# A decoder trunk on one core: q, k and v formed in pairs by seven block products for eight, with h and N kept in DRAM meanwhile

## The chip, the cores and the metric

The kernel runs on one core of one Trainium2 chip. The metric is the time of one execution on the device in microseconds (us). A core has five engines that work beside each other, each through a queue of its own in order: TensorE (PE; PEld is its loading of weights), VectorE (DVE), ScalarE (ACT), GpSimd (POOL) and SyncE (SP), which here only issues transfers. SBUF is the core's working memory, PSUM the accumulators into which TensorE writes, in banks of 128 x 512 float32, and DRAM the chip's memory. Transfers (DMA) run beside all engines.

## What is computed

A trunk of two layers on 1024 positions of width 1024, in float32. Layer 0 mixes positions by a gated MLP on chunks, layer 1 by dilated attention; each is followed by a squared-ReLU MLP of width 4096, with RMSNorm ahead of each part and at the end. The attention is what the change touches: 8 heads of 64, each in three dilation groups, so q, k and v have 3 × 3 × 512 = 4608 columns.

```python
WINDOW_DILATIONS = ((128, 1), (512, 4), (2048, 16))

def _dilated_attention_mixer(h, w_qkv, w_out, rel_bias):
    qkv = (h @ w_qkv).astype(jnp.float32).reshape(B_, S_, 3, N_DIL_GROUPS, ATT_HEADS, HEAD_DIM)
    for g, (window, dil) in enumerate(WINDOW_DILATIONS):
        n_, d_, m_ = _dilated_group(qkv[:, :, 0, g], qkv[:, :, 1, g], qkv[:, :, 2, g],
                                    rb[:, g * ATT_HEADS:(g + 1) * ATT_HEADS], window, dil)
        ...
    o = (num_sum / den_sum[..., None]).astype(h.dtype).reshape(B_, S_, ATT_WIDTH)
    return o @ w_out
```

A group's query attends to keys at its dilation, with a bias by distance; the groups' numerators are added with factors from their maxima and denominators, and the projection `o @ w_out` is added to h.

## The kernel before

**Products.** A float32 operand is split into a high and a low part (ScalarE copies, `split` L201; VectorE subtracts), and each product is three matmuls: high·high, high·low, low·high (`three` L354, `mm` L212). Tiles are 128 columns of weights by 512 positions, a half; a product over all 1024 inputs is 8 blocks, or 24 matmuls, into one PSUM bank. There are three banks for products, `mm`, and others, `at`, for scores, transposes and sums.

**Seven for eight.** The MLPs multiply 2 × 2 blocks by seven products in the manner of Strassen and Winograd. `Terms` (L407) makes the seven combinations of the normed input: `first` for half 0, `second` for half 1, with four combinations on the way, `rest` the splits of the others. `Weights` (L365) loads four blocks of 128 x 512, combines them on GpSimd and splits seven results. `product` (L359) runs one of the seven, 4 blocks or 12 matmuls. Attention does not use this before the change.

**Attention.** Twelve units, head pairs `hp` 0 to 3 by groups in the order 1, 2, 0, have three tiles each, q, k and v: 36 tiles. `unit_qkv` (L991) loads each tile's weights as two transfers and two splits (`weight` L205) and forms it with `both` (L344), 2 halves × 8 blocks × 3 matmuls; the first three tiles are formed `lagged` (L331), side by side, while the norm still runs. `out` takes q and k from PSUM as high (ScalarE) and low parts (VectorE), v as a ScalarE copy that `v_side` transposes. Scores, softmax, transposes and values of the unit before (`attention`, L1114) run between these products, four steps a unit. `merge` (L1201) joins the groups of a head pair, `split_N` splits the result into `o`, and for head pairs 0 and 1 `project_side` projects it at once: 8 tiles a half, 3 matmuls each, `add_h` after each. Head pairs 2 and 3 are projected at the end of the stage, summed in PSUM. h, the residual, stays in SBUF all along (8 tiles of 128 x 1024).

**The order.** PE's order is written by hand: the program keeps a model clock (`Flow`) and, after each product of a block (`flow.pump`), starts those pieces of side work whose due time has come, with waits from the table `LAT` (for example 4200 ns from scores to the transposes of their softmax, 3800 from these to the values). The other engines' orders come from a scheduler with priorities. All loads and stores of this part stand in SP's queue in order; loads of weights go through four buffers `r`, each free once its splits have read it.

## Time and profile before

| | |
|---|---|
| median of three runs | 2202.95 us (2201.97 to 2206.11) |
| span of the profiled execution | 2201.6 us |
| PE, DVE, ACT, POOL busy in it | 98%, 71%, 50%, 23% |
| layer 0, MLP | about 400 to 900 us |
| start of attention | 930 to 985 us |
| attention | 985 to 1511 us |
| its last output tiles | 1511 to 1545 us |
| start of layer 1's MLP | 1545 to 1615 us |

The profile is of one execution. Its page gives the busy time of each engine over the span, the span in 40 slices (digits are tenths), the chain of work that ended last, and groups of like instructions. From the trace come tables by stretch of time, timelines, and lists of what an engine waited for. In a name such as `mm<-y,whi` the output stands before the arrow; L179 is a line of the kernel above. A matmul's listed duration overlaps with its neighbours', so the time that one takes is read from the chain or from starts.

### The profile page before, as it was taken

The numbers are of one execution on the slowest core, as the hardware profiler recorded it, in microseconds if no ns is written. First come the engines' busy times: TensorE is split into PE (matmuls) and PEld (weight loads), VectorE is DVE, ScalarE is ACT, GpSimd is POOL, SyncE is SP. The second block draws the span as 40 slices with busy tenths as digits, with TensorE's granted clock in tenths as the row PEclk, the third lists the DMA queues.
The fourth block names the chain that finished last, engine by engine and source line by source line (L and its number), as shares of the span: only waits on it lengthen the run. The fifth ranks groups of instructions, "written<-read, shape, count | busy, mean of one in ns | idle before, by whom it ended". The sixth has DMA issues, their size and how long they took to land.

```text
span 2201.6 us, 30359 instructions
## 1 busy us (share of the span) xinstructions
PE 2153.2 (98%) x10402; PEld 1781.1 (81%) x10402; DVE 1556.9 (71%) x2844; ACT 1109.3 (50%) x2237; POOL 510.6 (23%) x375
## 2 busy tenths in 40 slices
PE   8999999999999999999999999999999999999998
PEld 6888887888878888778888888887778888788887
DVE  6875268776688887775664754647987777988866
ACT  6744135555564443356544545555555556544433
POOL 1100124333223333510000000001443332432345
PEclk9999999999999999999999999999999999999999
DMA  6321104444355443311111111120154443644432
GB/s 220 108 75 52 45 22 159 158 154 148 125 179 162 152 154 115 106 31 40 44 41 44 35 41 49 31 45 20 39 177 153 155 146 128 197 148 150 149 91 96
DMA packets 152335, 230.29 MB, mean 105 GB/s; under 512 B 32761, under 2 KB 47220, under 8 KB 152180
## 3 DMA queue, kind: packets, MB, share of 16 engines
q1 hardware_dynamic: 151280, 227.11, 32.9%
q8 instruction: 82, 1.34, 0.3%
q10 hardware_dynamic: 900, 1.23, 0.2%
q14 instruction: 73, 0.60, 0.1%
HBM read 170.45 MB, written 57.84 MB: 104 GB/s over the span
## 4 chain that ended last, share of the span: by engine, by line
PE 86%; DVE 6%; ACT 2%; DMA 2%; issue 2%; POOL 1%; SPq 0%; DVEq 0%; POOLq 0%; ACTq 0%
PE mm L179 43%; PE at L179 41%; PE at L186 2%; DVE wp L203 1%; DVE y L203 1%; DVE h L818 0%; DVE t L203 0%; ACT t L1072 0%; DMA r<-in_w_dn 0%; DMA t<-in_b_s 0%; DVE h L327 0%; ACT wp L202 0%; DVE b L444 0%; DMA t<-in_w_dl 0%; DMA r<-in_w_v 0%
## 5 line engine op out<-in xcount | busy, mean ns | idle before, releaser
L179 PE MATMUL mm<-y,whi 128*128 128x512 f32 x1616 | 507.8, 395 | 1.0 <-DVE h L327 1.0
L202 ACT ACTIVATE wp<-r 128x512 fp32r<-128x512 f32 (+3 forms) x388 | 232.0, 600 | 403.6 <-PE at L179 230.5
L179 PE MATMUL at<-hx,wp 128*128 128x512 f32 x1770 | 414.4, 390 | 2.5 <-DVE h L818 2.5
L179 PEld LDWEIGHTS at<-hx,wp 128*128 128x128 f32 x1770 | 333.0, 188 | 73.5 <-DVE h L818 4.2
L203 DVE TENSOR_TENSOR wp<-r,wp 128x512 fp32r<-128x512 f32 (+3 forms) x388 | 323.8, 838 | 83.8 <-ACT wp L202 81.0
L179 PEld LDWEIGHTS mm<-y,whi 128*128 128x128 f32 x1616 | 296.4, 188 | 62.9 <-DVE h L327 1.4
L179 PE MATMUL mm<-y,wlo 128*128 128x512 f32 x808 | 315.4, 390 | 0.0
L179 PE MATMUL at<-t,wp 128*128 128x512 f32 x1344 | 314.5, 389 | 0.8 <-DVE wp L203 0.8
L179 PEld LDWEIGHTS at<-t,wp 128*128 128x128 f32 x1344 | 252.1, 188 | 54.0 <-DVE wp L203 1.2
L256 POOL TENSOR_TENSOR t<-t 128x512 f32<-128x512 f32 (+1 forms) x60 | 78.1, 1301 | 869.6 <-ACT t L251 858.0
L384 POOL TENSOR_TENSOR t<-r 128x512 f32<-128x512 f32 (+3 forms) x62 | 91.2, 1470 | 606.2 <-DMA r<-in_w_up 192.6
L179 PE MATMUL mm<-y,wp 128*128 128x512 f32 x912 | 223.0, 390 | 0.4 <-DVE y L203 0.2
L179 PEld LDWEIGHTS mm<-y,wp 128*128 128x128 f32 x912 | 170.7, 188 | 37.5 <-issue 0.6
L179 PE MATMUL mm<-hx,wp 128*128 128x512 f32 x708 | 172.4, 390 | 6.7 <-DVE b L839 4.4
L179 PEld LDWEIGHTS mm<-y,wlo 128*128 128x128 f32 x808 | 151.7, 188 | 33.1
L203 DVE TENSOR_TENSOR wlo<-r,whi 128x512 fp32r<-128x512 f32 x160 | 113.4, 730 | 74.0 <-ACT whi L202 74.0
L179 PEld LDWEIGHTS mm<-hx,wp 128*128 128x128 f32 x708 | 132.6, 188 | 35.9 <-ACT wp L202 5.0
L202 ACT ACTIVATE whi<-r 128x512 fp32r<-128x512 f32 x160 | 97.0, 626 | 121.5 <-PE mm L179 90.0
L203 DVE TENSOR_TENSOR hx<-t,hx 128x512 fp32r<-128x512 f32 x192 | 141.8, 742 | 0.5 <-ACT hx L202 0.5
L818 DVE TENSOR_TENSOR h<-h,at 128x512 f32<-128x512 f32 x144 | 97.8, 682 | 55.8 <-PE at L179 55.6
L179 PE MATMUL at<-y,wp 128*128 128x512 f32 x480 | 120.6, 394 | 4.8 <-ACT t L715 4.1
L202 ACT ACTIVATE hx<-t 128x512 fp32r<-128x512 f32 x192 | 119.4, 630 | 6.6 <-DMA t<-hid 2.0
(205 smaller groups left out, 3052.6 us busy)
## 6 DMA issues: line engine op xcount, KB each, us to landing
t<-hid SPq DMA_DIRECT2D x182, 256.0 KB, 3.2
hid<-t SPq DMA_DIRECT2D x140, 256.0 KB, 2.3
r<-in_w_up SPq DMA_DIRECT2D x128, 256.0 KB, 2.7
r<-in_w_dn SPq DMA_DIRECT2D x88, 256.0 KB, 2.6
r<-in_w_qkv SPq DMA_DIRECT2D x72, 256.0 KB, 2.7
hid<-b SPq DMA_DIRECT2D x56, 256.0 KB, 2.3
r<-in_w_v SPq DMA_DIRECT2D x48, 256.0 KB, 3.2
h<-in_xT SPq DMA_DIRECT2D x16, 256.0 KB, 5.9
```

The lines of the kernel that those rows point to most:

```text
L179: nc.tensor.matmul(out, lhsT, rhs, **kw)
L186: nc.tensor.transpose(out, src, ident)
L202: nc.scalar.activation(hi, src, AF.Copy)
L203: nc.vector.tensor_tensor(lo, src, hi.bitcast(F32), op=ALU.subtract)
L256: nc.gpsimd.tensor_tensor(self.acc, self.acc, sq, op=ALU.add)
L384: tt(r3, r[0, 0], r[1, 0], op=ALU.subtract)
L818: engine.tensor_tensor(hs[i, s], hs[i, s], src, op=ALU.add)
```

## The change

The first four tiles, (unit 0: q, k, v) and (unit 1: q), are formed by a plain loop, `classical`, taken out of the MLP's code. The 32 others go in 16 pairs through `seven`: seven products of 12 matmuls, with 4 loads, 5 GpSimd combinations and 7 splits of weights, a ScalarE copy and five VectorE additions to put the results together. The normed input is held as `Terms`. A unit's q, k and v thus come in pairs that can span two units, and the values of the last unit wait for both its parts of V.

Meanwhile h is stored to DRAM (`hd`) after `xa.rest()`, its tiles now come from the pool `slots` (38 buffers for 28), and the merged numerators N of head pairs 0 to 2 are stored too (`kept_N`). In the last pair, after its product 1, `ahead_of_last` loads N, splits it into `o`, loads the projection's weights, loads h, and projects head pairs 0 to 2 of half 0: 8 tiles of 9 matmuls, summed in PSUM, each with one `add_h`. Half 1's follow with head pair 3, 12 matmuls a tile. There are 11 temporaries `t` for 8.

```diff
-    slots = ctx.enter_context(tc.tile_pool(name="slots", bufs=28))
+    slots = ctx.enter_context(tc.tile_pool(name="slots", bufs=38))
...
-        return tpool.tile([P, HALF], F32, tag="t", name="t")
+        return tpool.tile([P, HALF], F32, tag="t", name="t", bufs=NT)
...
-    h = [const.tile([P, S], F32, name=f"h{k}") for k in range(KT)]
+    h = [slot(name=f"h{k}") for k in range(KT)]
...
+    def seven(w, x, more, put_out, begun=None):
+
+        a = mm_bank()
+        product(a, w[1], x.t[1])
+        more()
+        if begun:
+            begun()
+        u = temp()
+        with tc.high_priority(offset=PRIO):
+            nc.scalar.activation(u, a, AF.Copy)
+        b = mm_bank()
+        product(b, w[6], x.t[6])
+        more()
+        with tc.high_priority(offset=PRIO):
+            nc.vector.tensor_tensor(u, u, b, op=ALU.add)
+        d = mm_bank()
+        product(d, w[5], x.t[5])
+        more()
+        c22 = temp()
+        with tc.high_priority(offset=PRIO):
+            nc.vector.tensor_tensor(c22, u, d, op=ALU.add)
+        e = mm_bank()
+        product(e, w[7], x.t[7])
+        more()
+        put_out(1, 1, c22, e, True)
+        product(d, w[3], x.t[3], True)
+        more()
+        put_out(0, 1, u, d)
+        product(a, w[2], x.t[2], True)
+        more()
+        put_out(0, 0, a)
+        product(e, w[4], x.t[4], True)
+        more()
+        put_out(1, 0, u, e, True)
...
-            yield (u.v if x else u.v_first), 0
+            yield u.v, 0
             if x == 0:
-                for s in range(2):
-                    split_N(2, s)
                 u.N = slot(name="N")
...
+        if hp < 3:
+            if i == 0:
+                kept_N[hp] = dram.tile([P, S], F32, tag=f"N{hp}", name=f"N{hp}", bufs=1)
+            nc.sync.dma_start(kept_N[hp][:, half(i)], N)
+        else:
+            split_N(hp, i, N)
...
+    def ahead_of_last():
+
+        N = [slot(name="N") for _ in range(3)]
+        for hp in range(3):
+            nc.sync.dma_start(N[hp], kept_N[hp])
+        yield 4000
+        for hp in range(3):
+            for i in range(2):
+                split_N(hp, i, N[hp][:, half(i)])
+                yield 900
+            proj_load(hp)
+            yield 900
+        for k in range(KT):
+            h[k] = slot(name=f"h{k}")
+            nc.sync.dma_start(h[k], hd[k])
         for m in range(8):
             b = mm_bank()
-            proj_mm(hp, i, m, b, True, True)
-            add_h(m, half(i), b)
-            yield 900
-        projected[hp, i].t = flow.t
-        if i == 1:
-            del wbo[hp]
...
+            for hp in range(3):
+                proj_mm(hp, 0, m, b, hp == 0, hp == 2)
+            add_h(m, half(0), b)
+            yield 0
+        three_done.t = flow.t
+
+    quads = [((1, 1), (1, 2))]
+    for i in range(2, NU, 2):
+        quads += [((i, 1), (i, 0)), ((i, 2), (i + 1, 0)), ((i + 1, 1), (i + 1, 2))]
...
+    xa.rest()
+    hd = [dram.tile([P, S], F32, tag=f"hd{k}", name=f"hd{k}", bufs=1) for k in range(KT)]
+    for k in range(KT):
+        nc.sync.dma_start(hd[k], h[k])
+
+    for n, two in enumerate(quads):
+        wn = Weights(qkv(*quads[n + 1])) if n + 1 < len(quads) else None
+        more = ahead(wn)
+        more()
...
+        seven(w, xa, more, lambda i, *x: out(two[i], *x), None if wn else lambda: flow.add(ahead_of_last()))
+        w = wn
+    half_done.t = flow.t
```

`out_v` and `out_qk` do what `out` did, after adding the two summands where there are two.

How this moves instructions is shown at three places. The first is PE's order from the transposes of the last unit's first softmax (`at<-ident,t`) to its values (`at<-p,V`). Before, with products of v (`mm<-y`) between them:

```order
L186 MATMUL at<-ident,t 128x128 x8
...
L186 MATMUL at<-ident,t 128x128 x4
L179 MATMUL mm<-y,whi 128x512 x2
...
L186 MATMUL at<-ident,t 128x128 x8
L179 MATMUL at<-p,V 128x256 x2
...
L186 MATMUL at<-ident,t 128x128 x12
L179 MATMUL mm<-y,whi 128x512 x2
```

and with the change, where the rows on top are the last projections of half 0 (`mm<-o`) and the last two blocks of the last product:

```order
L180 MATMUL mm<-o,whi 128x512 x2
L180 MATMUL mm<-o,wlo 128x512
L180 MATMUL mm<-t_8802,wp 128x512 x3
L180 MATMUL mm<-t_8810,wp 128x512 x3
L187 MATMUL at<-ident,t 128x128 x6
L180 MATMUL at<-k_13960,q_13640 128x256 x2
...
L187 MATMUL at<-ident,t 128x128 x8
...
L187 MATMUL at<-ident,t 128x128 x16
L180 MATMUL at<-p,V 128x256 x2
```

All products stand ahead of the first transposes now, and only transposes, scores and values follow.

The second is SP's queue at the end of attention, where `r<-in_w_bo` are the projection's weights, `r<-in_w_up` the first of the next MLP, and `sc` and `ex` the exchange of the last softmax's sums. Before:

```order
L168 DMA r<-in_w_bo 128x512
L168 DMA r<-in_w_up 128x512 x4
L925 DMA t<-bvec 128x2x256
L1194 DMA sc_13722<-st_13441 512x1x4 x2
L168 DMA r<-in_w_bo 128x512 x2
L1196 DMA ex_13725<-sc_13722 128x8x4
L168 DMA r<-in_w_up 128x512 x4
```

and with the change, where `N_10022` and the like lie in DRAM, as does `hd`:

```order
L1358 DMA N<-N_10022 128x1024
...
L169 DMA r<-in_w_bo 128x512 x2
L169 DMA r<-in_w_up 128x512 x2
L1251 DMA sc_13858<-st_13520 512x1x4 x2
L169 DMA r<-in_w_up 128x512
L1253 DMA ex_13861<-sc_13858 128x8x4
L169 DMA r<-in_w_up 128x512
L169 DMA r<-in_w_bo 128x512 x2
L1368 DMA h_14024<-hd_8813 128x1024
L1368 DMA h_14026<-hd_8814 128x1024
```

The eight loads of h stand behind those of w_bo and of the first w_up.

The third is VectorE's order there, with the change: `h_14024<-h_14024,mm` is the add to the first tile of h, L1129 a step of the last unit's softmax, `wp<-r,wp` a split of w_up, and `p<-at,p` the split of the first transposes.

```order
L328 TENSOR_TENSOR h_14026<-h_14026,mm 128x512
L1129 ISA t,st_14051<-at,b 128x256
L1129 ISA st_14051 128x1
...
L204 TENSOR_TENSOR wp<-r,wp 128x512 x2
L328 TENSOR_TENSOR h_14034<-h_14034,mm 128x512
L204 TENSOR_TENSOR wp<-r,wp 128x512
L328 TENSOR_TENSOR h_14036<-h_14036,mm 128x512
L328 TENSOR_TENSOR h_14038<-h_14038,mm 128x512
L1009 TENSOR_TENSOR t<-t,mm 128x512
L204 TENSOR_TENSOR wp<-r,wp 128x512
L204 TENSOR_TENSOR p<-at,p 128x384 x2
```

The last unit's first split of transposes comes behind all eight adds to h.

More of the change, by code (lines that the diff above doesn't have):

```diff
@@ L398, in ahead, with plain @@
         return lambda: next(it, None)
[L400 removed]
+    def plain(src):
         w = {}
@@ L403, in plain, with up, classical @@
             for i in range(2):
-                w[i, j] = wpair().split(load(w_up[layer, q, i, j]))
+                w[i, j] = wpair().split(load(src(i, j)))
         return w
+    def up(layer, q):
+        return lambda i, j: w_up[layer, q, i, j]
+    def classical(x, first, s, banks):
+        order = [(j, k) for j in range(2) for k in range(4)] if s == 0 else [(j, k) for k in range(4) for j in range(2)]
+        for n, (j, k) in enumerate(order):
+            xs = x.blocks[j, s]
+            flow.until(lambda: len(xs) > k)
+            for t, b in enumerate(banks):
+                three(b, first[t // 2][t % 2, j], blk(k), xs[k], n == 0, n == 7)
+                flow.pump()
     class Terms:
@@ L640, in trunk @@
                 if s == 0:
-                    first = [plain(0, q) for q in range(2)]
+                    first = [plain(up(0, q)) for q in range(2)]
     hidden = {}
@@ L686, in mlp @@
                 banks = [mm_bank() if n < 3 else at_bank() for n in range(4)]
[L687 to L693 removed]
+            classical(x, first, s, banks)
             for b, (q, i) in zip(banks, tiles):
@@ new lines, in trunk @@
+    quads = [((1, 1), (1, 2))]
+    for i in range(2, NU, 2):
+        quads += [((i, 1), (i, 0)), ((i, 2), (i + 1, 0)), ((i + 1, 1), (i + 1, 2))]
+    flow.add(attention())
+    for s in range(2):
+        banks = [at_bank() if (n < 2) == (s == 1) else mm_bank() for n in range(4)]
+        if s == 0:
+            banks = [mm_bank() if n < 3 else at_bank() for n in range(4)]
+        classical(xa, firsts, s, banks)
+        if s == 1:
+            U[0].bias = bias_tile(U[0].hp, U[0].g)
+        for b, tile in zip(banks, ((0, 0), (0, 1), (0, 2), (1, 0))):
+            out(tile, s, b)
+        if s == 0:
+            w = Weights(qkv(*quads[0]))
+            for _ in w.steps():
+                pass
```

193 lines of the change are left out of this document (98 added, 95 removed).

## The prediction

> **What bounds the kernel now.** I read the page first: busy times, slices and the chain of work that ended last.
>
> ```profile
> span 2201.6 us, 30359 instructions
> PE 2153.2 (98%) x10402; PEld 1781.1 (81%) x10402; DVE 1556.9 (71%) x2844; ACT 1109.3 (50%) x2237; POOL 510.6 (23%) x375
> PE   8999999999999999999999999999999999999998
> PE 86%; DVE 6%; ACT 2%; DMA 2%; issue 2%; POOL 1%; SPq 0%; DVEq 0%; POOLq 0%; ACTq 0%
> ```
>
> TensorE works in 98% of the span, no slice but the ends lets it rest, and 86% of the chain is its own. So a matmul that goes is time that goes, unless something else takes its place. Its price is read from the chain, in a piece without a stall:
>
> ```profile
> 402.46 5.44 PE at L179 x24
> ```
>
> 24 matmuls of 512 columns in 5.44 us are 0.2267 us each.
>
> Then I cut the span into its stages (columns: stretch, length, busy time of PE, PEld, DVE, ACT, POOL with instruction counts, granted clock, DMA share, GB/s). In this order they are: layer 0's up and down products (two rows each way of a hand-over), the start of attention in two pieces, attention, its last output tiles in two, and the start of layer 1's MLP.
>
> ```profile
> 400.00:620.00 220.00, 220.00 (x972) 182.15 (x971) 157.56 (x197) 119.77 (x207) 66.59 (x45) 1.00 0.44 144
> 620.00:660.00 40.00, 35.79 (x148) 28.23 (x147) 35.34 (x56) 23.63 (x48) 14.08 (x13) 0.96 0.60 191
> 660.00:900.00 240.00, 240.00 (x1061) 198.79 (x1060) 191.31 (x264) 105.52 (x172) 84.42 (x60) 1.00 0.47 143
> 930.00:960.00 30.00, 28.43 (x137) 23.07 (x136) 24.93 (x46) 13.16 (x24) 9.55 (x8) 1.00 0.05 10
> 960.00:985.00 25.00, 24.61 (x120) 20.03 (x119) 14.71 (x28) 12.66 (x18) 0.00 (x0) 1.00 0.14 36
> 985.00:1511.00 526.00, 523.40 (x3070) 437.96 (x3068) 302.19 (x889) 281.31 (x769) 0.00 (x0) 1.00 0.15 41
> 1511.00:1521.00 10.00, 5.72 (x31) 4.39 (x32) 9.94 (x15) 5.79 (x11) 0.00 (x0) 0.93 0.20 52
> 1521.00:1530.00 9.00, 9.00 (x37) 8.29 (x37) 3.03 (x7) 2.41 (x6) 0.00 (x0) 0.51 0.01 2
> 1545.00:1600.00 55.00, 52.28 (x234) 42.23 (x235) 52.27 (x73) 29.84 (x54) 24.37 (x17) 1.00 0.13 40
> 1600.00:1615.00 15.00, 12.30 (x49) 9.76 (x48) 14.47 (x18) 9.96 (x19) 7.18 (x5) 0.89 0.58 217
> ```
>
> In attention, 985 to 1511, PE works 523.4 of 526 us; VectorE 302 (57%), ScalarE 281 (53%), GpSimd not at all. The other stages, which form their products by seven for eight already, have VectorE at 72% and 80% of 220 and 240 us, GpSimd at 30% and 35%, and PE without a gap. Only at 620 to 660, with VectorE at 88%, does PE lose 4.2 us of 40.
>
> **The matmuls: −43.5 us.** A tile costs 2 halves × 8 blocks × 3 passes = 48 matmuls. 32 tiles are 1536. A pair by seven products is 7 × 4 blocks × 3 passes = 84, and 16 pairs are 1344. The instruction lists agree: 512-column matmuls go from 8474 to 8282. 192 × 0.2267 = 43.5 us off the chain. Of the output projections none goes: 2 head pairs × 2 halves × 8 tiles × 3 = 96 matmuls, 21.8 us, only move from among the products to the end of attention. That stage should therefore last 526 − 43.5 − 21.8 = 461 us before any new wait.
>
> **VectorE in that stage: +5 us.** These rows are groups of attention (columns: line, engine, operation, output and inputs, count, then busy us, mean ns, idle before):
>
> ```profile
> L203 DVE TENSOR_TENSOR wlo<-r,whi 128x512 fp32r<-128x512 f32 x65 | 44.3, 687 | 53.2 <-ACT whi L202 53.2
> L327 DVE TENSOR_TENSOR h<-h,mm 128x512 f32<-128x512 f32 x32 | 21.8, 684 | 12.0 <-PE mm L179 11.8
> L1029 DVE SCALAR_TENSOR_TENSOR q<-mm,q 128x512 fp32r<-128x512 f32 x22 | 21.2, 965 | 10.7 <-ACT q L1028 10.7
> ```
>
> and these of layer 0's up products, 400 to 620, the last of layer 0's down products, 660 to 900:
>
> ```profile
> L203 DVE TENSOR_TENSOR wp<-r,wp 128x512 fp32r<-128x512 f32 x65 | 53.5, 823 | 30.9 <-ACT wp L202 30.9
> L667 DVE TENSOR_TENSOR t<-t 128x512 f32<-128x512 f32 x11 | 18.4, 1676 | 0.0
> L384 POOL TENSOR_TENSOR t<-r 128x512 f32<-128x512 f32 x10 | 17.6, 1762 | 112.5 <-DMA r<-in_w_up 67.7 <-DVE wp L203 44.8
> L742 DVE TENSOR_TENSOR t<-t,at 128x512 f32<-128x512 f32 x12 | 8.2, 687 | 8.4 <-PE at L179 8.4
> ...
> L203 DVE TENSOR_TENSOR wp<-r,wp 128x512 fp32r<-128x512 f32 x66 | 62.7, 950 | 1.0
> ```
>
> Off: 64 weight splits × 0.687 = 44 us, 32 adds to h × 0.684 = 22. On: 7 splits a pair, 112 × 0.823 to 0.950 = 92 to 106; 5 adds of an output from PSUM a pair, 80 × 0.687 = 55. So 302 − 66 + 147 to 161 = 383 to 397 us, or 83 to 86% of 461. Per pair, 84 × 0.2267 = 19.0 us of products stretch with attention's own matmuls to 461 / 16 = 29 us, in which GpSimd has 5 additions of at most 1.762 us, 31%. ScalarE gains a copy a pair and 3 splits more, and stays below VectorE. What VectorE is late with holds PE in two ways: a PSUM bank of the three is needed again one product (12 × 0.2267 = 2.7 us) after its add was asked for, and the softmax of attention stands in the same queue. The bounds: 0, as at 660 to 900 with 80%; and the 10.5% lost at 620 to 660 with 88%, over 461 us, 48. The stage lies between these; I take 5, near the lower end, since 620 to 660 is a hand-over between two stages that waits for first operands, and the 461 us are a steady stream.
>
> [...]
>
> **The start of attention: +3 us.** At 930 to 985 PE works 53.04 of 55 us: 2.0 lost, to the last sums of h and the norm. The new start forms terms and their combinations, as layer 1's MLP does at 1545 to 1615, where VectorE is at 95% of the first 55 us and PE loses 2.7 + 2.7 = 5.4 us. 5.4 − 2.0 = 3.4, which I take as 3; bounds 0 and 4. It runs beside nothing else but four plain tiles, so nothing hides it.
>
> **The end of attention: +4 us.** The last unit's transposes, scores and values have filler between them now. Its PE timeline (start, length; in brackets the idle time ahead and its cause):
>
> ```profile
> 1497.36 0.82 PE L186 MATMUL at<-ident,t 128*128 128x128 f32 x6
> 1498.11 0.97 PE L179 MATMUL at<-k,q 64*128 64x256 f32 x12
> 1499.01 1.09 PE L186 MATMUL at<-ident,t 128*128 128x128 f32 x8
> ...
> 1501.77 0.71 PE L179 MATMUL mm<-y,whi 128*128 128x512 f32 x2
> ...
> 1503.93 1.03 PE L186 MATMUL at<-ident,t 128*128 128x128 f32 x8
> 1504.72 2.49 PE L179 MATMUL at<-p,V 128*128 128x256 f32 x20
> 1507.05 1.50 PE L186 MATMUL at<-ident,t 128*128 128x128 f32 x12
> 1508.30 0.70 PE L179 MATMUL mm<-y,whi 128*128 128x512 f32 x2
> ...
> 1512.04 0.66 PE L186 MATMUL at<-ident,t 128*128 128x128 f32 x4 [1.41 <-ACT t L1229]
> 1512.45 0.70 PE L179 MATMUL mm<-o,whi 128*128 128x512 f32 x2
> ...
> 1519.05 0.50 PE L179 MATMUL mm<-o,whi 128*128 128x512 f32 x1 [2.26 <-ACT o L202]
> ...
> 1520.53 0.80 PE L179 MATMUL mm<-o,whi 128*128 128x512 f32 x1 [0.98 <-DVE o L203]
> ```
>
> From the first transposes at 1497.4 to the split o of the last head pair at 1520.5 are 23.2 us, 4.65 of them idle. In the changed order all projections of half 0 stand ahead of those transposes, and between the two points are left 46 transposes (0.12 each), 24 scores (0.9 per 12) and 44 value products (2.33 per 20): 12.5 us. The chain of softmax, transposes, values, merge and split is the same. If it ran through the three fillers (2.2 us from 1501.8, 2.3 from 1508.3, 2.4 from 1512.45) it lasts 23.2 still and leaves 10.7 idle, 6 more than now; if each of them delayed it, 16.3 and 3.8, 1 less. I take 2 more. Half clock comes on top: 0.51 over 1521 to 1530, where 4.5 of 9 us are lost already; longer gaps may draw it out by as much again, and I take 2. Bounds −1 and 6 + 4.5 = 10.5.
>
> [...] The longest gap in the rows above is 2.26, and the clock still fell; what went ahead was a stretch with PE at 5.72 of 10 us. [...]
>
> **h and N through DRAM: +2 us.** Their transfers are priced by these rows (count, KB each, us to landing; then a stretch at full DMA):
>
> ```profile
> h<-in_xT SPq DMA_DIRECT2D x16, 256.0 KB, 5.9
> r<-in_w_qkv SPq DMA_DIRECT2D x72, 256.0 KB, 2.7
> 1605.00:1610.00 5.00, 4.45 (x20) 3.36 (x18) 4.80 (x7) 2.21 (x5) 3.33 (x3) 1.00 0.97 368
> ```
>
> Storing h after the terms are formed is 8 × 512 KB = 4.2 MB, at 10 to 41 GB/s of other traffic: hidden behind the first pair's 29 us, and 4.2 MB / 217 GB/s = 19 us if it were not. N is 6 stores of 256 KB, far apart: nothing. Reading h back is what can be late. It is asked for after product 1 of the last pair and after the splits of o, on SP's queue behind w_bo and the first w_up, whose buffers come free only with VectorE's splits. 4.2 MB take 11.4 us at 368 GB/s, 19 at 217, 43 as 16 × 2.7 one by one. Its cover is 72 matmuls of projections, 16.3 us, and each of the 8 adds to h frees the bank that the second next tile needs. Behind those adds on VectorE stand the last unit's softmax steps and its splits, so a late h delays the tail itself. The first of 8 tiles is enough to begin, so I take 2; bounds 0 and 43 − 16.3 = 27, of which I hold 20 likely at most. The end of the stage is the one place where a late transfer of this change isn't covered by 400 us of products.
>
> **The sum.** −43.5 + 5 + 3 + 4 + 2 = −29.5 on the span of 2201.6: 2172.1. The median shown, 2202.95, lies 1.35 above that span; with this, 2173.5, told as 2174.
>
> **The rivals.**
>
> *All of it hidden.* VectorE at 83 to 86% still feeds PE, as at 80%, and h lands in time: −43.5 + 3 or so, 2157 to 2166, say 2161. For: PE without a gap over 460 us of the same kind of products. Against: those stages had no softmax in VectorE's queue, and the tail had little slack before the change.
>
> *h comes late.* The chain w_up buffers, h, adds, banks, softmax in order on VectorE costs 20 rather than 2, and the tail's clock falls: 2174 + 18 = 2192, 2184 to 2200. For: SP issues in order and the r buffers are four. Against: DMA is at a share of 0.15 there.
>
> *VectorE becomes the bound of attention: slower.* If GpSimd's additions make the 112 splits cost 1.676 rather than 0.950, that adds 81 us, and 397 + 81 = 478 us no longer fits in 461. With 5% of hand-overs lost the stage takes 503, 42 more; with start and end 2202.95 − 43.5 + 42 + 9 = 2210. Slower begins where the stage exceeds 461 + 43.5 − 9 = 495 us, with 478 us of VectorE in it. Against: the 950 ns were taken with GpSimd at 35% already, more than the 31% here. For: the low parts of q and k (965 ns from PSUM) and their sums now meet GpSimd too.
>
> That the change does less than it says is excluded by the counted matmuls.
>
> **How the numbers follow.** The forecast 45% (its own range 2166 to 2184), all hidden 22%, h late 18%, VectorE the bound 15%. The range is 2156 to 2204: below, 2202.95 − 43.5 − 2.6 (all of attention's idle time too) is 2157; above, it takes in late h and the beginning of the fourth case, leaving out about 11%. A measurement of this kernel tells about 0.2%, 4.4 us, from no change. Faster by more is 45 + 22 + 16 of the late h + 1 of the fourth = 84%; within it 2 + 2 = 4%; slower 12%.
>
> **What would show it.** The count of 512-column matmuls lower by 192, or the first term falls. In attention VectorE at 83 to 86% and GpSimd at a quarter to a third, with PE's waits for adds and splits summing to some 5 us; well over 20 would be the fourth case. At the start, waits of PE for terms of 5 us in place of 2. From the last unit's first transposes to its split o, idle time of 5 to 8 and a clock of about 0.5 behind it. PE waiting for the adds to h and these for the transfer of h, over 5 us, would be the third case. The forecast is wrong if the splits take over 1.2 us on average, or if h lands over 10 us after its first projection is summed.

## The result and the profile after

The changed kernel takes 2210.78 us, the median of 6 runs (2203.96 to 2212.53), against 2202.90 for the kernel before beside it: a ratio of 1.0029, 95% interval 1.0015 to 1.0042. It is slower by 0.3%, where 2174 was forecast, and above the range. The page of its profiled execution shows why this is a puzzle (the span; busy time of the engines; PE's 40 slices; the chain by engine):

```profile
span 2210.2 us, 30177 instructions
PE 2130.3 (96%) x10210; PEld 1756.5 (79%) x10210; DVE 1665.1 (75%) x2978; ACT 1136.6 (51%) x2294; POOL 613.2 (28%) x448
PE   7999999999999999979999999998999999999998
PE 78%; DVE 12%; ACT 4%; issue 2%; DMA 2%; POOL 1%; SPq 0%; DVEq 0%; POOLq 0%; ACTq 0%
```

The 192 matmuls are gone (10402 to 10210), and PE still works in 96% of the span. But the chain that ended last has 78% of PE in it, not 86%, and 12% of VectorE for 6%. VectorE is never near full over the span. The stage tells more. From the first sums of attention's norm (`at<-ones`) to the first product of the next MLP's w_up, the table of stretches of the kernel before reads (columns as in the prediction: busy time of PE, PEld, DVE, ACT, POOL, then granted clock, DMA share, GB/s)

```profile
932.67:1550.35 617.68, 608.48 (x3470) 508.00 (x3470) 370.14 (x1007) 325.79 (x841) 21.16 (x16) 0.99 0.14 37
1000.00:1490.00 490.00, 487.93 (x2832) 408.92 (x2832) 276.79 (x788) 254.20 (x684) 0.00 (x0) 1.00 0.15 40
```

and that of the changed one, the stage as a whole, the steady middle, the tail, from the last unit's first transposes to its split o, and the start:

```profile
936.77:1561.66 624.89, 584.38 (x3278) 481.94 (x3277) 483.81 (x1156) 365.59 (x908) 131.80 (x91) 0.96 0.19 57
1010.00:1480.00 470.00, 449.79 (x2638) 373.05 (x2639) 360.59 (x923) 287.78 (x755) 89.01 (x60) 0.98 0.19 51
1505.07:1526.83 21.76, 16.55 (x118) 14.71 (x116) 18.03 (x52) 14.13 (x38) 0.00 (x0) 0.84 0.00 1
936.77:983.60 46.83, 35.07 (x163) 27.92 (x161) 43.99 (x68) 22.76 (x37) 20.76 (x15) 0.91 0.30 112
```

The stage is 7.2 us longer (624.9 − 617.7), most of the 8.6 between these two executions; what stands ahead of it takes 4.1 us more and what follows 2.7 less. PE's idle time in it went from 9.2 to 40.5 us: 11.8 at the start, 20.2 in the middle, 5.2 in the tail and 3.3 elsewhere. The clock adds to it: busy time × (1 − granted clock), summed over stretches of 2 us, is 4.7 us before and 17.6 after. What is left, the work itself at full clock, fell from 603.8 to 566.8, by 37. So 37 us of work went, 31.3 of idle time and 12.9 of half clock came: −37 + 31 + 13 = +7.

Of the 43.5 us forecast for the matmuls 6.5 are not found. Some of these are the waits' own: a matmul's listed 0.39 us covers 0.16 us in which the next could have started (0.39 − 0.2267), so each wait hides up to 0.16 us in busy time. PE's timeline lists 24 more waits than before between 900 and 1630 (41 for 17), up to 3.9 us. The account itself is good to some 3 us only: for the same number of matmuls e11 below finds 46.8 less. The rest isn't located.

What PE waited for, 930 to 1630 (waiting, what ended it: us in total, times, longest):

```profile
PE mm L180 <- DVE q L1050: 11.3, 1, 11.3
PE at L187 <- ACT t L1286: 4.3, 3, 2.7
PE at L180 <- DVE tr L204: 3.8, 4, 2.1
PE at L180 <- ACT tr L203: 3.2, 1, 3.2
PE at L187 <- ACT t L1131: 2.5, 4, 1.5
PE at L180 <- ACT q L1049: 2.5, 1, 2.5
```

One wait of 11.3 us, and then many of up to three. None names a transfer of h: the loads landed at 401 GB/s over 1485 to 1494 while PE worked all of these 9 us, and over 1470 to 1530 PE waited 0.2 us for an add to h.

```profile
1485.00:1494.00 9.00, 9.00 (x56) 6.92 (x55) 6.52 (x27) 4.35 (x18) 0.00 (x0) 1.00 1.01 401
```

Each of the seven gaps of 1.51 us and more between 930 and 1560 is followed by half clock in this execution. In PE's timeline (start, length; in brackets the gap and what ended it) and in the stretches behind three of the gaps:

```profile
983.61 1.65 PE L180 MATMUL mm<-y,wp 128*128 128x512 f32 x3 [11.35 <-DVE q L1050]
1050.48 1.24 PE L187 MATMUL at<-ident,t 128*128 128x128 f32 x3 [1.51 <-ACT t L1131]
1254.69 0.69 PE L180 MATMUL at<-k,q 64*128 64x128 f32 x4 [2.46 <-ACT q L1049]
1477.22 0.47 PE L180 MATMUL at<-tr,V 128*128 128x128 f32 x1 [3.22 <-ACT tr L203]
```

```profile
1053.00:1056.00 3.00, 3.00 (x9) 2.30 (x9) 1.03 (x9) 1.65 (x8) 0.00 (x0) 0.50 0.27 87
1257.00:1260.00 3.00, 3.00 (x10) 2.52 (x11) 2.49 (x10) 1.63 (x6) 0.00 (x0) 0.50 0.00 0
1479.00:1482.00 3.00, 3.00 (x10) 2.52 (x9) 2.18 (x5) 1.44 (x3) 0.00 (x0) 0.50 0.66 193
```

PE is fully busy here with 9 or 10 matmuls in 3 us; at 0.2267 us for the largest it would do 13.

### The profile page after: what moved, and what is told of

Read it like the earlier page. It is cut to its first block, busy times and chain, and to the rows that moved or that the text cites. A ratio compares the mean times of both kernels' runs of the same rounds, so it can differ in the third digit from the quotient of the medians.

```text
span 2210.2 us, 30177 instructions
## 1 busy us (share of the span) xinstructions
PE 2130.3 (96%) x10210; PEld 1756.5 (79%) x10210; DVE 1665.1 (75%) x2978; ACT 1136.6 (51%) x2294; POOL 613.2 (28%) x448
## 3 DMA queue, kind: packets, MB, share of 16 engines
q8 instruction: 80, 1.31, 0.2%
## 4 chain that ended last, share of the span: by engine, by line
PE 78%; DVE 12%; ACT 4%; issue 2%; DMA 2%; POOL 1%; SPq 0%; DVEq 0%; POOLq 0%; ACTq 0%
PE at L180 39%; PE mm L180 37%; DVE wp L204 2%; PE at L187 2%; DVE y L204 1%; ACT t L1131 1%; DVE t L204 1%; DVE tr L204 1%; DVE h L826 1%; DVE q L1050 1%; ACT wp L203 1%; DVE N L1169 1%; DVE h L328 0%; DMA r<-in_w_v 0%; DMA r<-in_w_up 0%
## 5 line engine op out<-in xcount | busy, mean ns | idle before, releaser
L203 ACT ACTIVATE wp<-r 128x512 fp32r<-128x512 f32 (+3 forms) x492 | 296.4, 605 | 427.4 <-PE at L180 186.9
L204 DVE TENSOR_TENSOR wp<-r,wp 128x512 fp32r<-128x512 f32 (+3 forms) x492 | 390.8, 798 | 128.2 <-ACT wp L203 125.3
L180 PE MATMUL mm<-y,wp 128*128 128x512 f32 x1608 | 402.5, 396 | 14.9 <-DVE q L1050 11.3
L180 PEld LDWEIGHTS mm<-y,wp 128*128 128x128 f32 x1608 | 300.2, 189 | 82.2 <-DVE q L1050 11.8
L385 POOL TENSOR_TENSOR t<-r 128x512 f32<-128x512 f32 (+3 forms) x78 | 106.3, 1362 | 883.5 <-DMA r<-in_w_up 253.5
L180 PE MATMUL mm<-t,wp 128*128 128x512 f32 x768 | 195.3, 402 | 0.0
L180 PEld LDWEIGHTS mm<-t,wp 128*128 128x128 f32 x768 | 143.4, 192 | 31.2
L204 DVE TENSOR_TENSOR hx<-t,hx 128x512 fp32r<-128x512 f32 x192 | 164.9, 871 | 1.2 <-ACT hx L203 1.1
L180 PE MATMUL mm<-y,whi 128*128 128x512 f32 x512 | 158.3, 390 | 0.0
L387 POOL TENSOR_TENSOR r<-r 128x512 f32<-128x512 f32 (+3 forms) x78 | 117.3, 1504 | 76.2 <-DVE wp L204 71.6
L390 POOL TENSOR_TENSOR r<-r 128x512 f32<-128x512 f32 (+3 forms) x78 | 107.9, 1383 | 109.1 <-issue 72.0
L180 PEld LDWEIGHTS at<-y,wp 128*128 128x128 f32 x552 | 104.2, 189 | 23.0 <-issue 1.3
```

The source lines that it names most:

```text
L180: nc.tensor.matmul(out, lhsT, rhs, **kw)
L203: nc.scalar.activation(hi, src, AF.Copy)
L204: nc.vector.tensor_tensor(lo, src, hi.bitcast(F32), op=ALU.subtract)
L385: tt(r3, r[0, 0], r[1, 0], op=ALU.subtract)
L387: tt(r[1, 1], r[1, 0], r[0, 0], op=ALU.subtract)
L390: tt(r[0, 0], r[0, 1], r[1, 1], op=ALU.subtract)
```

## The experiments

Four causes could make these waits. **Late starters**: a few operations stand in an in-order queue behind work that arrives late, each is one gap, and moving it gives the gap back. **GpSimd**: its additions slow VectorE's, or are themselves late. **VectorE's throughput**: too much work for the stage. **The chain of attention itself**: product, add, split, scores, softmax, transposes, values take as long one after the other as the products between which they are laid, so that PE waits wherever products get shorter. The first two are local and cheap to undo; the last would mean that there were never 43.5 us to win. Every version ran in five rounds beside the kernel before; ratios are to it, with 95% intervals. The stage's account (length, PE's idle time, half-clock loss, work at full clock) is worked out for one profiled execution each as above; single executions of one kernel differ by up to some 12 us, so small differences are read from the medians.

| kernel | median us | ratio | length | idle | half clock | work |
|---|---|---|---|---|---|---|
| before | 2202.9 | 1 | 617.7 | 9.2 | 4.7 | 603.8 |
| the change | 2210.78 | 1.0029 (1.0015 to 1.0042) | 624.9 | 40.5 | 17.6 | 566.8 |
| e1_start | 2199.49 | 0.9983 (0.9971 to 0.9995) | 614.4 | 31.9 | 14.9 | 567.6 |
| e2_exchange_pool | 2209.66 | 1.0023 (1.0011 to 1.0035) | 615.6 | 38.2 | 11.1 | 566.3 |
| e4_raw_weights | 2200.03 | 0.9982 (0.9971 to 0.9993) | 614.6 | 34.0 | 15.2 | 565.4 |
| e5_start_exchange | 2202.41 | 0.9992 (0.9983 to 1.0002) | 611.3 | 31.7 | 12.0 | 567.6 |
| e6_up_later | 2191.60 | 0.9952 (0.9939 to 0.9965) | 604.7 | 27.2 | 9.9 | 567.6 |
| e7_latencies | 2189.07 | 0.9938 (0.9921 to 0.9955) | 603.4 | 27.2 | 7.6 | 568.6 |
| e8_raw_on_e6 | 2185.20 | 0.9921 (0.9908 to 0.9934) | 598.9 | 23.5 | 9.7 | 565.7 |
| e9_adds_on_dve | 2194.18 | 0.9963 (0.9949 to 0.9976) | 610.6 | 27.3 | 16.2 | 567.1 |
| e10_filler | 2193.71 | 0.9946 (0.9934 to 0.9958) | 607.4 | 26.0 | 13.2 | 568.1 |
| e11_six | 2187.81 | 0.9921 (0.9907 to 0.9935) | 597.4 | 48.3 | 28.4 | 520.8 |
| e12_no_low | 2183.56 | 0.9903 (0.9886 to 0.992) | 596.7 | 20.7 | 10.8 | 565.2 |
| e13_six_no_low | 2165.70 | 0.983 (0.9812 to 0.9848) | 580.3 | 37.5 | 22.7 | 520.1 |

### The gap at the start: e1_start

VectorE's timeline of the changed kernel in the 11.35 us gap:

```profile
976.58 1.28 DVE L204 TENSOR_TENSOR y<-r,y 128x512 fp32r<-128x512 f32 x2
977.79 0.68 DVE L457 TENSOR_TENSOR b<-r,keep 128x512 f32<-128x512 f32 x1
978.57 0.69 DVE L458 TENSOR_TENSOR b<-r,b 128x512 f32<-128x512 f32 x1
979.18 3.43 DVE L204 TENSOR_TENSOR t<-b,t 128x512 fp32r<-128x512 f32 x2
982.53 1.02 DVE L1050 SCALAR_TENSOR_TENSOR q<-mm,q 128x512 fp32r<-128x512 f32 x1
```

The first tiles of half 0 end on PE at 972.3. Their banks come free only with the low parts of q and k (L1050), and these stand in VectorE's queue behind all terms of half 1 (`second`), the last of them two splits at 979.2 to 982.5. VectorE has no gap here; it is the order that is wrong. The edit spaces `second`'s steps so that the low parts come ahead of its last quarter, and takes its temporaries from another pool so that they can:

```diff
-            start_terms(sq, 1, 2, xa)
+            flow.add(xa.second(sq, 2, 7000.0, temp), LAT["sum"])
...
-                    t = raw()
+                    t = room()
...
-                yield 2 * LAT["tile"]
+                yield step
```

> The steps of half 1's terms are set 7 us apart in the model clock (3.2 before) and take temporaries in place of load buffers, so that VectorE's order has the low parts of the first q and k tiles ahead of the last quarter of the terms. Theory A (the loss is a handful of stalls, each with its own late item in an in-order queue, and half clock behind it): the gap of 11.35 us before the matmul at 983.6 falls below 2 us, the half clock behind it (some 3 us) goes too, and the time falls from 2210.8 by 11 to 15 us, to 2196 to 2200. Theory B (VectorE is simply too full, so that a stall taken away here comes back later): the gap moves into half 1's products or the first pair, and the time stays within 4 us of 2210.8.

Measured: 2199.49; the ratio falls by 0.0046, 10 us, from 1.0029 to 0.9983; 2196 to 2200 was expected. PE's timeline shows what is left of the gap:

```profile
973.16 0.96 PE L180 MATMUL mm<-y,wp 128*128 128x512 f32 x3 [0.68 <-ACT t L1007]
975.96 1.49 PE L180 MATMUL mm<-y,wp 128*128 128x512 f32 x3 [1.83 <-DVE q L1050]
```

2.5 us of 11.35 remain. A late starter: shown, with its price.

### The exchange of sums on another queue: e2_exchange_pool and e5_start_exchange

The read of the exchanged sums stands in SP's queue behind loads of weights. Here it is issued from GpSimd's queue (with the program's scratch space for dynamic transfers raised from 1024 to 2048); e5 has this and the edit of e1.

```diff
-        nc.sync.dma_start(e.rearrange("p b a c -> p b (a c)"), sc.rearrange("(b p) v -> p b v", p=P))
+        nc.gpsimd.dma_start(e.rearrange("p b a c -> p b (a c)"), sc.rearrange("(b p) v -> p b v", p=P))
```

> The read-back of the softmax sums (ex<-sc) is issued on GpSimd's queue in place of SP's, so that SP does not stand still until the store has landed. Theory A: the wait of VectorE for the bias load (3.2 us before 1045) and of ScalarE for w_up (3.4 us before 1476) go, with the PE gaps of 1.8 and 3.5 us and some 3 us of half clock behind each: 8 to 11 us, 2200 to 2203. Theory B (these waits were no cause, or they return elsewhere): within 4 us of 2210.8. A third way: issuing costs GpSimd so much that the weights come late, over 2214.

> Both of the first two edits at once. Theory A: the gains add, 19 to 26 us, 2185 to 2192, below the kernel before by 11 to 18. Theory B: no more than the better of the two, and not below 2200.

Measured: 2209.66 and 2202.41. The first is the changed kernel's time again, the second not below e1 alone (0.9992 against 0.9983, intervals overlapping). The gaps that it was to take away are still there in e2's timeline, 3.27 us before the transposed probabilities `tr` at 1470.7 and 1.31 before 1048.9. ScalarE's wait for w_up ahead of that `tr`, which was to go, is still there too, 3.49 us before 1469.8. The place of the exchange in SP's queue is not what PE waits for. Both lie 7 to 17 us above what was expected if it were, and fit the other case; the profiled execution of e2 (span 2199.5) is 9 us below its median, so its row in the table flatters it.

### The split of w_up ahead of a split of transposes: e6_up_later

ScalarE's timeline of the changed kernel at the 3.2 us gap:

```profile
1476.26 0.63 ACT L203 ACTIVATE wp<-r 128x512 fp32r<-128x512 f32 x1 [3.44 <-DMA r<-in_w_up]
1476.80 0.37 ACT L203 ACTIVATE tr<-at 128x256 fp32r<-128x256 f32 x1
```

ScalarE waits 3.44 us for a transfer of w_up, the next MLP's weights, to split it, and the high part of `tr`, which PE needs, stands behind it in the same queue. (`tr` are the transposes of the unit before the last; those of the last unit are called `p`.) The list of waits blames `ACT tr`; the row ahead of it on ScalarE shows that it is a DMA. e6 is e1 with the first w_up asked for one step later, behind the projection's last weights and the last o:

```diff
-        if i == 0:
-            first = [plain(up(1, 0))]
         proj_load(3)
         flow.until(lambda: (3, i) in outs)
+        if i == 0:
+            first = [plain(up(1, 0))]
```

> On top of the start edit, the first splits of the next MLP's weights (w_up) are written behind the wait for the last o, so that ScalarE no longer stands before a load of w_up with a split of the last unit's transposes behind it. Theory A: the PE gap of 3.2 + 0.45 us before 1468 and the half clock behind it (3 us) go, 5 to 7 us below the start edit alone (2199.5): 2192 to 2195. Theory B (the gap is only the first of several late items at that place): within 2 us of 2199.5.

Measured: 2191.60, 0.9952, 6.8 us below e1 by the ratios and just below the 2192 to 2195 expected; the gap is gone, and its price fits what the changed kernel lost there, 3.5 us idle and 3.3 of half clock behind it. With these two moved operations the change is faster than the kernel before by 0.5%.

### GpSimd: e4_raw_weights, e8_raw_on_e6 and e9_adds_on_dve

In e4, made from the changed kernel, and in e8, made from e6, the weights of the pairs go to the splits uncombined, so GpSimd has nothing to do in the middle of the stage; the kernel leaves out the combining. In e9, e6 again, the additions are made on VectorE. There are four of them a pair (L385, L386, L387 and L390 of the changed kernel), not the five that the prediction and the expectations count, and all three edits, like e12's below, reach the 15 pairs after the first: e9 has 60 GpSimd instructions less and 60 VectorE instructions more than e6.

```diff
+            if self.raw:
+                self.split(4, r[1, 1])
+                yield
+                self.split(1, r[0, 0])
+                yield
+                for p, src in ((5, r[1, 0]), (6, r[1, 1]), (7, r[0, 0]), (3, r[0, 0]), (2, r[0, 1])):
+                    self.split(p, src)
+                    yield
+                return
```

```diff
-            r, tt = self.r, nc.gpsimd.tensor_tensor
+            r, tt = self.r, (nc.vector if self.on_dve else nc.gpsimd).tensor_tensor
```

> The weights of the sixteen pairs are split uncombined: GpSimd's five additions a pair are left out, all else stands. The kernel so leaves out the combining of the weights. If GpSimd's work is what slows VectorE and ScalarE's chain (contention, 31% of the stage): q's low part falls from 1182 to about 970 ns, the steps of 128x8 that took 1.2 us fall to 0.16, and PE's gaps of 19 us between 1040 and 1505 fall below 9, time 10 to 16 us lower, 2195 to 2201. If the gaps come from the order and from late transfers (theory A): the 128x8 steps get short, but most gaps stand, time 2 to 7 us lower.

> The first of these four with the combining of weights left out (five GpSimd additions a pair), as the raw weights were on the change itself. If contention with GpSimd is a cause of its own, independent of the start and of w_up, its 10 us come off again: 2182 to 2186. If it only worked through stalls that the two edits have taken away, under 4 us.

> The first of these four with the five additions a pair on VectorE in place of GpSimd: 80 x 0.685 = 55 us more on VectorE, 76% to about 88% of the stage, and no GpSimd work there. If contention and GpSimd's slow additions (1.3 to 1.6 us each) cost more than VectorE's share does: 3 to 10 us below the first. If VectorE's share is the limit (theory B): 10 us or more above it.

Measured: 2200.03 (10.4 us below the change, by the ratios), 2185.20 (6.8 below e6) and 2194.18 (2.4 above e6, intervals overlapping). The groups of VectorE's instructions, 1012 to 1480, of e6:

```profile
L204 DVE TENSOR_TENSOR wp<-r,wp 128x512 fp32r<-128x512 f32 x91 | 69.2, 763 | 36.5 <-ACT wp L203 35.6
L1050 DVE SCALAR_TENSOR_TENSOR q<-t,q 128x512 fp32r<-128x512 f32 x20 | 23.6, 1181 | 2.3 <-ACT q L1049 2.0
L1046 DVE TENSOR_TENSOR t<-t,mm 128x512 f32<-128x512 f32 x31 | 21.2, 685 | 6.3 <-PE mm L180 6.1
```

and of e8:

```profile
L204 DVE TENSOR_TENSOR wp<-r,wp 128x512 fp32r<-128x512 f32 x110 | 75.4, 688 | 41.7 <-ACT wp L203 41.2
L1060 DVE SCALAR_TENSOR_TENSOR q<-t,q 128x512 fp32r<-128x512 f32 x20 | 19.0, 949 | 3.5 <-ACT q L1059 3.2
L1056 DVE TENSOR_TENSOR t<-t,mm 128x512 f32<-128x512 f32 x31 | 21.2, 684 | 6.4 <-PE mm L180 6.2
```

With GpSimd at work a split takes 0.763 us and a low part of q 1.18; without it 0.688 and 0.949. The add from PSUM takes 0.685 either way. Contention is there for these two groups, whose inputs both lie in SBUF, but not for every such group (`k<-t,k` takes 0.975 in e6 and 0.974 in e8), and it is small on average: 105 × 0.075 = 8 us of VectorE's time for the splits. At one place it shows as a wait of PE. Two steps of the softmax's sums on VectorE, 0.16 us elsewhere, meet GpSimd's additions in the changed kernel:

```profile
1246.06 1.63 POOL L385 TENSOR_TENSOR t<-r 128x512 f32<-128x512 f32 x1 [22.45 <-DMA r<-in_w_qkv]
1246.45 1.26 DVE L1274 TENSOR_TENSOR dn<-f,st 128x8 f32<-128x8 f32 x1
1247.76 1.27 POOL L386 TENSOR_TENSOR r<-r 128x512 f32<-128x512 f32 x1
1247.82 1.24 DVE L1277 TENSOR_TENSOR dn<-dn,d 128x8 f32<-128x8 f32 x1
```

Each ends within 0.03 us of the addition that it met, and PE waits for the split of `tr` behind them in VectorE's queue (2.13 us before 1250.5; 2.06 in e6). Without GpSimd's work, in e4, e8 and e9, this wait is gone.

e4's time is in the range expected of contention, but PE's gaps between 1040 and 1505 only fall from 19.1 to 16.1 us, where under 9 was the sign of it; e8's is in that range too. e9 has the short durations (0.687 and 0.940), but VectorE does 60 additions more, PE's waits for q before scores grow from 3.7 us in e6 to 7.1, and its time is no better: it lies between the two cases expected. e8's gain can't be put down to the contention alone: it also leaves out the wait for the additions. What is shown is the size: all that GpSimd does to this stage is worth some 7 us on top of e6, known to some 4 by the two intervals.

### The steps' due times: e7_latencies and e10_filler

e7 is e6 with longer due times in the model clock, so that scores, transposes and values stand later in PE's order:

```diff
-LAT = dict(... soft=4200.0, turn=3800.0, fe=1300.0, v=2000.0, qk=2700.0, ...)
+LAT = dict(... soft=4400.0, turn=4000.0, fe=1300.0, v=2600.0, qk=4700.0, ...)
```

e10 is e7 with the projections of half 0 from the third on 3 us apart, as filler for the tail:

```diff
-            yield 0
+            yield 3000 if m >= 2 else 0
```

> On top of that the model's latencies are raised: 4700 ns for q and k (2700), 4400 for the softmax (4200), 4000 for transposes (3800), 2600 for v (2000), so that PE's order asks for them later. If the small gaps come from an order that asks too early for results with a longer chain (an add ahead of each q, k and v): the gaps of 0.3 to 2.5 us before scores, transposes and values between 1000 and 1460 (some 16 us) halve, and the time falls by 6 to 12 us to 2182 to 2188. If attention's own chain is what paces the stage now (products wait for the scores of the unit before), the waits only move ahead of the products, and the time stays or rises by up to 8.

> On top of the raised latencies, the projections of half 0 from the third tile on are set 3 us apart in the model clock, so that they stand between the last unit's transposes, scores and values instead of ahead of them. Theory A (the tail loses because it has no filler): the gaps of 2.7 and 1.6 us before the merge's transposes and the o of the last head pair, and the half clock behind them, go: 4 to 8 us below the raised latencies (2189.1), 2181 to 2185. If the last unit's own chain sets the end, the projections only delay it: 0 to 4 us above.

Measured: 2189.07 and 2193.71. e7 gains 3 us where 6 to 12 were expected (intervals overlap): between 1000 and 1460 the listed waits did not halve, they are 25 with 16.8 us for 20 with 15.1, and the stage's idle time stayed 27.2. It has the lowest median of the versions that compute all. e10 is 1.8 us above e7 by the ratios, as expected if the last unit's own chain sets the end: the filler takes the wait before the last head pair's projections, but idle time falls by 1.2 only, since waits are longer elsewhere (3.1 us for the next norm's sums, where e7 has 1.9), and half clock goes from 7.6 to 13.2. The medians' intervals overlap; a gain from this filler is not seen.

### What TensorE's time is worth now: e11_six, e12_no_low and e13_six_no_low

To see what limits the stage once TensorE's work is cut, cut it further. e11 is e6 without the last of the seven products, e12 is e6 without the low parts of the pairs' weights on VectorE, and e13 is both.

```diff
-        product(e, w[4], x.t[4], True)
         more()
         put_out(1, 0, u, e, True)
...
+            if self.hi_only:
+                w = self.w[p] = self.place()
+                nc.scalar.activation(w.hi, src, AF.Copy)
+                w.lo = w.hi
+                return
             self.w[p] = self.place().split(src)
```

> On top of the w_up edit (2191.6), the last of the seven products is left out in each of the sixteen pairs, with its split weights formed as before: 192 matmuls fewer, as many as the change itself took away. The kernel so leaves out that product. If TensorE is still the bound of attention, 192 x 0.2267 = 43.5 us go: 2148 to 2156. If attention's own chain (scores, softmax, transposes, values) or VectorE has become the bound, under 25 us go: above 2167.

> On top of the w_up edit (2191.6), the low parts of the weights of all sixteen pairs are left out on VectorE: 112 splits x 0.77 = 86 us less there, while TensorE runs as many matmuls (the third pass reads the high part) and ScalarE and GpSimd work as before. If VectorE's queue is what makes attention's results late: the idle time of 27 us and the 10 us of half clock in the stage fall to 15 and under 5, and the time by 12 to 20 us, to 2172 to 2180. If the latency of attention's own steps paces the stage, whatever VectorE has beside them: under 6 us.

> The same with the last product of each pair left out too, as in the run with six products (2187.8, only some 7 us below the kernel that it was made from). If VectorE was the bound there: 192 x 0.2267 = 43.5 us off the run without the low parts, nearly whole: 30 to 43 us below it. If attention's chain was the bound: 0 to 15 us below it.

Measured: 2187.81, 2183.56 and 2165.70. The middle of the stage, first of e6, then of e11, e12 and e13:

```profile
1010.00:1480.00 470.00, 455.39 (x2680) 378.31 (x2680) 364.59 (x941) 288.99 (x760) 82.76 (x56) 0.99 0.21 60
```

```profile
1010.00:1480.00 470.00, 435.56 (x2579) 360.77 (x2578) 374.55 (x992) 301.25 (x800) 83.98 (x58) 0.96 0.21 60
```

```profile
1010.00:1480.00 470.00, 461.02 (x2731) 384.25 (x2729) 302.04 (x857) 293.67 (x773) 79.03 (x57) 0.99 0.22 62
```

```profile
1010.00:1480.00 470.00, 442.43 (x2647) 369.89 (x2645) 322.68 (x911) 306.51 (x809) 76.80 (x56) 0.96 0.21 61
```

A second 192 matmuls less, the same 43.5 us as in the change, bring 6.8 us by the ratios (0.9952 to 0.9921). The work falls by 46.8 us; idle time rises by 21.1 and half clock by 18.5. So TensorE's work no longer sets the end. VectorE is part of what does: with the low parts' 105 × 0.763 = 80 us of its work away (15 pairs of seven splits; 64% busy in e12's middle instead of 78% in e6's, 364.6 of 470) the time falls by 10.8, between the 12 to 20 expected if its queue is the cause and the under 6 if not. But its throughput alone does not bind, for with VectorE at 69% in e13 the 192 matmuls still bring only 16 us, from 0.9903 to 0.983. PE's longest waits there, 930 to 1600:

```profile
PE at L180 <- DVE V L1004: 12.0, 4, 3.4
PE mm L180 <- ACT o L203: 4.9, 1, 4.9
PE at L180 <- DVE k L1056: 3.4, 4, 1.1
PE at L187 <- DVE tr L204: 3.0, 4, 2.0
```

These are the links of attention's chain, V and k a few us after the product that forms them, `tr` after the transposes. The due times of the order are fixed lengths; with fewer products between them they come before their operands are there. That longer due times would help here was not tried. How much of the rest is the chain's own length and how much its place in VectorE's queue, these runs do not separate: 16 of 43.5 us lies just above the 0 to 15 expected of the chain.

## Why the prediction was wrong, step by step

**The matmuls, −43.5: right in number, and nearly in time.** 192 went; work at full clock fell by 37 us in the change, and by 46.8 and 45.1 for the same number in e11 and e13. Up to 3.9 of the missing 6.5 may be time hidden behind waits, as worked out above.

**VectorE in that stage, +5 (bounds 0 to 48): the step that failed.** Its work was sized right: 392 us over 985 to 1505, where 383 to 397 were said. The groups of VectorE's instructions, 1012 to 1505 of the changed kernel:

```profile
L204 DVE TENSOR_TENSOR wp<-r,wp 128x512 fp32r<-128x512 f32 x97 | 74.2, 767 | 42.6 <-ACT wp L203 41.7
L1046 DVE TENSOR_TENSOR t<-t,mm 128x512 f32<-128x512 f32 x31 | 21.2, 685 | 6.5 <-PE mm L180 6.3
```

The splits took 0.767 us (0.823 to 0.950 assumed), the adds from PSUM 0.685 (0.687), and VectorE is at 77% of the middle (83 to 86), since the stage did not get shorter. GpSimd is at 19% (31), with four additions a pair and not five. What failed is how the wait was priced: by VectorE's share of busy time, with "the 461 us are a steady stream" as the reason for the lower end. They are not a stream. Layer 0's products at 80% ran without a gap; attention has a chain whose every link passes through VectorE or ScalarE, and whose links stand at fixed distances in PE's order. The middle lost 20.2 us of 470 idle where 2.1 of 490 were lost before, and 10.4 of half clock behind three of its gaps: 28.5 where 5 was taken, inside the bounds, and the largest error of the sum. Taken apart by the runs: about 7 us from the split of w_up ahead of `tr` on ScalarE (e6), some 7 from GpSimd (e8), and the rest from the chain and VectorE's queue, of which 80 us less of VectorE's work gives back 10.8 (e12). That 10.8 and GpSimd's 7 were taken from the same kernel and not together, so they may overlap.

**The start of attention, +3 (bounds 0 to 4): the second step that failed.** 11.8 us idle and, behind the gap from 983.6 to 989, 2.8 of half clock, where 2.0 were lost before. (The 0.91 shown for 936.77 to 983.60 is idle time at half clock; it cost nothing.) The bound came from layer 1's MLP, which begins with the same terms but lost 2.7 us of 55 there. Here q and k of half 0 stood behind the terms. VectorE at much the same share (94%, and 95% there) costs 2.7 us or 11.35; e1, which changes the order in its queue and not its work, gives 10 back with the same work.

**A queue that was passed over.** The sum had the loads of w_up on SP's queue, as delay of h. It had nothing for the splits of w_up on ScalarE, and what stands behind them there. In the kernel before no wait of PE for `tr` is listed in this stage; in the changed one a `tr` of the unit before the last comes behind such a split. 6.8 us (e6).

**The end, +4: its signs came, its size did not.** From the last unit's first transposes to its split o PE idles 5.2 us (5 to 8 said), against 4.65 before. Half clock costs 2.8 us there, inside the stretch, and nothing behind the split o, where the kernel before loses 4.6. So by its own terms the end is 1.3 us cheaper than before, just below the lower bound of −1. Counted on to the first product of w_up it is 2.2 dearer, with a wait of 2.3 us for the next norm's sums and 1.7 of half clock behind it.

**h and N through DRAM, +2: no cost seen.** No wait of PE names a transfer of h, and the loads ran at 401 GB/s while PE worked. The third rival is out. That the trip costs nothing elsewhere wasn't tried by itself.

**The fourth rival had the time, 2210, and only part of the mechanism.** Its splits of 1.676 us did not come (0.767), VectorE had no 478 us of work (360.6 in 470), and it was not the bound. Contention with GpSimd is there, at a tenth of the split's time: in e6 and e8 763 against 688 ns for the splits, which read two tiles in SBUF, and 685 against 684 for the adds, with one input in PSUM. The forecast had named well over 20 us of waits for adds and splits as the sign of this case; the middle has 20.2 of all kinds, mostly from queue order and the chain. The right number by luck. Neither sign by which the forecast itself was to be known as wrong came: the splits took less than 1.2 us, and h was not late.

**The clock.** It was counted in the tail alone. The change has 12.9 us more of half clock, 17.6 at six places: behind the gap of 11.35 (2.8), at 1050 (3.4), 1252 (3.7), 1477 (3.3), in the tail at 1511 (2.8) and at 1542 (1.7), behind gaps of 1.5 to 3.2 us. The kernel before has one place in the stage, its tail.

So of the 43.5 us some 37 were won, and were turned into waits: about 10 at the start, 7 behind w_up, the rest in a stage whose second limit lay close behind the first. That the order could be mended is shown up to 2189.07 (e7, 0.9938, interval 0.9921 to 0.9955), which beats the kernel before by 14 us and the change by 20, by the ratios. What keeps it from the forecast 2174: its stage has 18.0 us more of idle time than before (27.2 against 9.2) and 2.9 more of half clock, where the forecast allowed 14 in all, and its work fell by 35 and not 43.5.

## What to carry to other kernels

Before pricing a cut on the engine that is 98% busy, ask what the stage would take if that engine were free: a copy with still less of its work (e11 here, made after the change) shows in one run that the second limit was near. In this kernel an engine's share of busy time did not price the waits: where a chain passes through it, look in its in-order queue for the late item (a last transfer, a last sum) and for what stands behind it, as with `second` ahead of q and `w_up` ahead of `tr`. The engine that the profile names as the cause of a wait may itself have stood before a transfer; read the row ahead of it. A gap on TensorE can cost more than its length: the stage's 31 us of added idle time brought 12.9 of half clock with them.

## What the runs showed of the hardware

In the changed kernel half clock came after gaps as short as 1.51 us (1050.48). PE was then fully busy at a granted clock of 0.50 from 1050.60 to 1057.42, with 1.00 ahead of this and behind it:

```profile
1047.18:1050.60 3.42, 1.67 (x8) 0.94 (x6) 2.85 (x12) 2.54 (x9) 0.74 (x1) 1.00 0.00 0
1050.60:1057.42 6.82, 6.82 (x25) 5.17 (x26) 3.98 (x14) 3.93 (x16) 0.00 (x0) 0.50 0.12 38
1057.42:1060.83 3.41, 3.41 (x23) 2.88 (x24) 1.40 (x4) 1.08 (x3) 0.00 (x0) 1.00 0.20 77
```

The length of the gap does not decide it. In the same execution a gap of 2.32 us stands ahead of the same matmuls in layer 0 and in layer 1, and only the second has half clock behind it:

```profile
656.49 2.32 PE L180 MATMUL mm<-hx,wp 128*128 128x512 f32 x9 [2.32 <-DVE t L847]
1906.90 3.81 PE L180 MATMUL mm<-hx,wp 128*128 128x512 f32 x9 [2.32 <-DVE t L847]
```

```profile
656.50:659.50 3.00, 3.00 (x13) 2.49 (x14) 3.00 (x6) 1.25 (x3) 0.00 (x0) 1.00 0.21 72
1906.90:1909.90 3.00, 3.00 (x8) 2.36 (x9) 3.00 (x6) 0.63 (x2) 0.00 (x0) 0.57 0.22 73
```

In e7 gaps of 1.73, 1.85 and 1.86 us had none behind them either, of which the last:

```profile
1356.42 0.66 PE L187 MATMUL at<-ident,t 128*128 128x128 f32 x4 [1.86 <-DVE tr L204]
1355.24:1357.24 2.00, 0.82 (x6) 0.79 (x7) 2.00 (x6) 0.00 (x0) 0.00 (x0) 1.00 0.00 0
1357.24:1359.24 2.00, 2.00 (x11) 1.64 (x10) 2.00 (x9) 1.91 (x7) 0.00 (x0) 1.00 0.01 4
```

What decides it isn't found.

Run to run, a kernel's time moved with the clock: of e1's executions one with a mean granted clock of 0.990 had a span of 2190.6, one with 0.987 a span of 2200.6, 10 us for the same instructions.
